# Value matmuls placed behind projection steps, norms cut in two, fill work at one rate over a chunk

## The chip, the cores and the metric

The kernel runs on one core of a Trainium2 chip. The metric is the device time of one execution in microseconds; the median of three runs is 2244.29 us (2243.23 to 2244.43). One further execution was recorded with the profiler and took 2247.89 us; its trace spans 2246.0 us, and every duration below comes from it.

## What is computed

Two layers over 2048 tokens of width 1024, between RMS norms. The even layer projects its input, attends over keys chosen by a top-256 index score (8 heads of 64), and runs a depthwise convolution of 31 taps with a layer norm beside it. The odd layer is a gated short convolution.

```python
def even_layer(h, pos, w_in, w_out, cb_w, cb_bias, ln_g, ln_b):
    u = h @ w_in
    q, k, v, qi, ki, wi, gate_a, glu_b, gate_b = _split(u, EVEN_SPLIT)
    ...
    a = dsa_attention(q, k, v, qi, ki, wi).reshape(Bn, S, ATT_WIDTH)
    a = a * jax.nn.silu(gate_a)
    ...
    c = causal_depthwise_conv(c, cb_w) + cb_bias
    c = jax.nn.silu(layer_norm(c, ln_g, ln_b))
    c = c * jax.nn.silu(gate_b)
    return jnp.concatenate([a, c], axis=-1) @ w_out

def odd_layer(h, w_in, conv_w, w_out):
    b_gate, c_gate, xin, gate = jnp.split(h @ w_in, 4, axis=-1)
    y = b_gate * causal_depthwise_conv(c_gate * xin, conv_w)
    return (y * jax.nn.silu(gate)) @ w_out

for l in range(DEPTH):
    h = rms_norm(x, norm_g[l])
    x = x + (even_layer(...) if l % 2 == 0 else odd_layer(...))
return rms_norm(x, final_g)
```

## The kernel before

Tokens are cut into four chunks of 512 (16 blocks of 128). Channels lie on partitions, tokens on the free axis. Every large product is made of three f16 matmuls (`mm3`, lines 179 to 183: high times high, high times low, low times high) over eight slices of the contraction, so one 128x512 result takes 24 matmuls. One projection step loads a 1 MB weight tile and makes two such results: 48 matmuls.

The program has two halves. The first (to about 856 us) projects the input of the even layer, scores and selects keys, and does the attention of chunk 0 and the convolution of chunk 0. The second goes chunk by chunk (the loop at line 1172). For a chunk `c` it runs 24 projection steps: 4 of `out_even(c)`, which need the attention and convolution of that chunk (tiles `mh`, `ml`; the attention fills slices 0 to 3 of the contraction, the convolution slices 4 to 7); 4 of `late`, which is `out_odd` of the chunk before; and 16 of `odd(c)`. Chunk 0 has its own first steps (lines 1112 to 1124), and its 16 steps of `odd` stand in the loop. Between the steps, `weave` (line 127) calls generators that emit other work: `attend(c + 1)`, one head of one block at a call (4 blocks of 8 heads make 32 calls, and a 33rd call retires what is left), and `conv(c + 1)`, which needs 16 calls. A rate says how many calls each step makes; a fraction is carried from step to step inside one `weave` and dropped at its end. R0, R1 and R2 are the rates of the attention, CN0 and CNR those of the convolution.

A head's work is a chain through every engine. TensorE makes the scores `ps_q` (`scores`, line 1148), in segments of 512 keys; VectorE adds the mask and keeps a running minimum (line 335); ScalarE takes the exponential (342) and casts (344); GpSimd makes the low part (345); SyncE issues one DMA transpose a segment (347, tile `pt`); then TensorE multiplies by the values (`values_of`, line 368, tile `ps_v`). The values of a head are emitted two calls after its scores (`LOOK` is 2). After the eighth head of a block, `end` (line 376) scales the result, transposes it on TensorE (390), multiplies by the gate (392) and splits it into `mh` and `ml`.

The order on each engine comes from a scheduler that works with a timeline of its own. It may place an instruction anywhere its inputs allow. `paced` (line 119) ties an instruction behind the last projection matmul emitted before the call (`state["gate"]`): it may not stand ahead of it on the engine. The first scores of a head are paced; the value matmuls are not. Each engine executes its instructions in the order given, and TensorE waits at a matmul whose inputs have not arrived.

`row_rstd` (line 152) makes a norm: four small matmuls sum squares, VectorE does a Newton iteration on 4 numbers, and one more matmul (line 163) spreads the result over the partitions.

Of the kernel before, what the change touches and what calls it, by code (L numbers as in the profile page):

```python
# [43 lines left out]
NWT = 2  # L44
LOOK = 2
ATR = 3.5
CE, CX, CN0, CNR, R0, R1, R2 = 1.5, 3.0, 1.0, 1.0, 2.0, 2.0, 2.5
ORDER = ('ggqgqg', 'ggqgqg', 'gggg', 'qq')
EX = 1
TQ, TP = 2, 4  # L50
# [23 lines left out]
def trunk_kernel(ctx: ExitStack, tc: tile.TileContext, xT, pos, wE, woE, wO, woO, par, tab, outT):  # L74
# [39 lines left out]
    w_dr = {}  # L114
    URGENT = {(wE.tensor.name, t) for t in (T_K, T_QI, T_KI)}

    state = {"mm": None, "gate": None, "scanned": False}

    def paced(ins):
        if state["gate"] is not None:  # L120
            tc.add_manual_dep(ins.ins, state["gate"].ins.name, mybir.DependencyInfo(mybir.DependencyClass.NoSync, mybir.DependencyReason.DATA), reason="pace")
# [5 lines left out]
    def weave(main, steps=99, *fills):  # L127
        owed = [0.0] * len(fills)
        for n, _ in enumerate(main):
            state["gate"] = state["mm"]  # L130
            for i, (gen, rate) in enumerate(fills):
                owed[i] += rate
                while owed[i] >= 1.0:
                    owed[i] -= 1.0
                    next(gen, None)
            state["gate"] = None
            if n + 1 == steps:
                break
# [11 lines left out]
        return r  # L150

    def row_rstd(pool, ps_pool, sq, inv_n, out_scale, n=TT):
        st = ps_pool.tile([P, CH], FP32, name="ps_m")
        for i in range(n):
            T.matmul(out=st[:, i:i + 1], lhsT=sq[:, i * P:(i + 1) * P], rhs=ones[:, 0:1], start=True, stop=True)
        a = pool.tile([P, TT], FP32, name="rs_a")[:, 0:n]
        V.tensor_scalar(out=a, in0=st[:, 0:n], scalar1=inv_n, scalar2=EPS, op0=ALU.mult, op1=ALU.add)
        r = newton_rsqrt(pool, a, [P, TT], "rs")[:, 0:n]
        dg = pool.tile([P, TT, P], FP32, name="rs_d", bufs=1)
        state["rstd"] = V.scalar_tensor_tensor(out=dg[:, 0:n, :], in0=id32.rearrange("p (o t) -> p o t", o=1).broadcast_to([P, n, P]), scalar=out_scale,  # L160
                                               in1=r.rearrange("p (i o) -> p i o", o=1).broadcast_to([P, n, P]), op0=ALU.mult, op1=ALU.mult)
        rb = ps_pool.tile([P, CH], FP32, name="ps_m")
        T.matmul(out=rb[:, 0:n * P], lhsT=ones, rhs=dg[:, 0:n, :].rearrange("p i t -> p (i t)"), start=True, stop=True)  # L163
        return rb

    def square_into(pool, acc, t, first, eng, tile=None):
# [12 lines left out]
    def mm3(out, sh, sl, mh, ml):  # L179
        for k in range(KD):  # L180
            T.matmul(out=out, lhsT=sh(k), rhs=mh(k), start=k == 0, stop=False)  # L181
            T.matmul(out=out, lhsT=sh(k), rhs=ml(k), start=False, stop=False)  # L182
            state["mm"] = T.matmul(out=out, lhsT=sl(k), rhs=mh(k), start=False, stop=k == KD - 1)  # L183

    def weight(pool, stage_pool, src, t):
        key = (src.tensor.name, t)
# [35 lines left out]
    def conv_norm(c, pool, aux, ps_pool, sink, sums=None):  # L222
        cv = pool.tile([P, NJ, CH], FP32, name="cv")
        s = pool.tile([P, CH], FP32, name="cn_s")
        cb, lng, lnb = pr("cb"), pr("lg"), pr("lb")
        for j in range(NJ):
            ci = pool.tile([P, CK - 1 + CH], FP32, name="cin")
            SP.dma_start(out=ci, in_=cg_dr[j][:, c * CH:c * CH + CK - 1 + CH])
            out = cv[:, j, :]
            acc = sums() if sums else out  # L230
            paced(A.activation(out=acc, in_=ci[:, 0:CH], func=AF.Identity, scale=cwt[:, j, 0:1], bias=cb[:, j:j + 1]))  # L231
            for t in range(1, CK):
                ins = V.scalar_tensor_tensor(out=out if t == CK - 1 else acc, in0=ci[:, t:t + CH], scalar=cwt[:, j, t:t + 1], in1=acc, op0=ALU.mult, op1=ALU.add)  # L233
                if t % 8 == 1:
                    paced(ins)
                if t % 8 == 0:
                    yield
            if j == 1:
                G.tensor_tensor(out=s, in0=cv[:, 0, :], in1=out, op=ALU.add)
            elif j > 1:  # L240
                G.tensor_tensor(out=s, in0=s, in1=out, op=ALU.add)
        mu = ps_pool.tile([P, CH], FP32, name="ps_m")
        T.matmul(out=mu, lhsT=inv512, rhs=s, start=True, stop=True)
        ssq = pool.tile([P, CH], FP32, name="cn_q")
        for j in range(NJ):
            V.tensor_tensor(out=cv[:, j, :], in0=cv[:, j, :], in1=mu, op=ALU.subtract)
            square_into(aux, ssq, cv[:, j, :], j == 0, G)
        with tc.high_priority(PRI):
            rb = row_rstd(aux, ps_pool, ssq, 1.0 / CW, 1.0)
        for j in range(NJ):  # L250
            x = cv[:, j, :]
            V.tensor_tensor(out=x, in0=x, in1=rb, op=ALU.mult)
            A.activation(out=x, in_=x, func=AF.Identity, scale=lng[:, j:j + 1], bias=lnb[:, j:j + 1])
            th = pool.tile([P, CH], FP32, name="cn_s")
            A.activation(out=th, in_=x, func=AF.Tanh, scale=0.5)
            V.scalar_tensor_tensor(out=x, in0=th, scalar=1.0, in1=x, op0=ALU.add, op1=ALU.mult)
            gb = pool.tile([P, CH], FP32, name="cn_q")
            SP.dma_start(out=gb, in_=gb_dr[c][:, j, :])
            V.scalar_tensor_tensor(out=x, in0=x, scalar=0.5 * SM, in1=gb, op0=ALU.mult, op1=ALU.mult)
            sink(j, x)  # L260
            yield
# [49 lines left out]
    def attention(blocks, tiles, scores, context, vv, eng, look, sink):  # L311
# [39 lines left out]
        def values_of(blk, h, parts):  # L351
            b, i = blk["b"], h % group
            if i == 0:
                state["av"] = context()
            if h == 0:
                blk["an"] = tiles["a"]()
                blk["ga"] = tiles["ga"]()
                SP.dma_start(out=blk["ga"], in_=ga_dr[b])
            av, an = state["av"], blk["an"]
            for kt, hi, lo in parts:  # L360
                if b < TT:
                    T.matmul(out=av, lhsT=hi, rhs=vv[:, kt, 0, :], start=kt == 0, stop=False)
                    T.matmul(out=av, lhsT=hi, rhs=vv[:, kt, 1, :], start=False, stop=False)
                    T.matmul(out=av, lhsT=lo, rhs=vv[:, kt, 0, :], start=False, stop=kt == b)
                    continue
                order = ((hi, 2 * HD), (lo, HD)) if kt == 0 else ((lo, HD), (hi, 2 * HD))
                for n, (p, w) in enumerate(order):
                    T.matmul(out=av[:, i, 0:w], lhsT=p, rhs=vv[:, kt].rearrange("p a d -> p (a d)")[:, 0:w], start=kt + n == 0, stop=kt == b and n == 1)  # L368
            if b < TT:
                A.copy(out=an[:, h, :], in_=av)  # L370
            elif i == group - 1:
                part = an[:, h - i:h + 1, :]
                A.copy(out=part, in_=av[:, :, 0:HD])
                V.tensor_tensor(out=part, in0=av[:, :, HD:2 * HD], in1=part, op=ALU.add)
# [643 lines left out]
                square_into(l1, acc, x1[:, jt, :], jt == 0, V)  # L1018
            yield

    def norm_odd(x1, acc):
        with tc.high_priority(PRI):
            return norm_all(x1, acc)

    def norm_all(x1, acc):
        rb = row_rstd(l1, ps_n, acc, 1.0 / D, SX)
        nh = l1.tile([P, KD, CH], F16, name="nh", bufs=1)
        nl = l1.tile([P, KD, CH], F16, name="nl", bufs=1)
        for k in range(KD):
            xn = l1.tile([P, CH], FP32, name="xi")  # L1030
            V.scalar_tensor_tensor(out=xn, in0=x1[:, k, :], scalar=g1[:, k:k + 1], in1=rb, op0=ALU.mult, op1=ALU.mult)
            split(nh[:, k, :], nl[:, k, :], xn)
        return nh, nl
# [86 lines left out]
    even = out_even(0, *m[0], x1, acc)  # L1120
    weave(even, EX, (cnv, CX))
    drain(even)
    n = norm_odd(x1, acc)
    drain(late)


# [45 lines left out]
    for c in range(NCH):  # L1172
        att = attend(c + 1) if c + 1 < NCH else iter(())
        if c > 0:
            cnv = conv(c + 1) if c + 1 < NCH else iter(())
            x1, acc = rows()
            weave(out_even(c, *m[c], x1, acc), 99, (cnv, CNR), (att, R0))
            n = norm_odd(x1, acc)
            weave(late, 99, (cnv, CNR), (att, R1))
        yh = l1.tile([P, KD, CH], F16, name="yh", bufs=1)  # L1180
        yl = l1.tile([P, KD, CH], F16, name="yl", bufs=1)
        weave(odd(*n, yh, yl), 99, (cnv, CNR if c else CN0), (att, R1 if c else R2))
        late = out_odd(c, x1, yh, yl, 2 if c + 1 == NCH else 1)
        drain(att)
        drain(cnv)
# [71 lines left out]
```

## Time and profile before

| | us |
|---|---|
| median of 3 runs | 2244.29 |
| profiled execution | 2247.89 |
| its span | 2246.0 |
| TensorE busy | 1994.7 |
| VectorE busy | 1657.6 |
| ScalarE busy | 1180.3 |
| GpSimd busy | 811.3 |

TensorE is busy for 89% of the span, the others for less. A matmul's recorded duration is longer than the distance to the next one, since matmuls overlap; idle time is what is read here. The second half consists of a stage for each chunk's steps: 932 to 1205 us (the 16 steps of `odd(0)`, with the attention of chunk 1), 1205 to 1553 us (24 steps, attention of chunk 2), 1553 to 1890 us (24 steps, attention of chunk 3), and a last one with no fill work.

### The profile page before, as it was taken

What the parts mean: (1) busy time and instruction counts of PE and PEld (TensorE: products, weight loads), DVE (VectorE), ACT (ScalarE), POOL (GpSimd) and SP (SyncE); (2) the same over time, 40 slices, a digit from 0 to 9 for tenths busy, and PEclk for the clock granted to TensorE, in tenths of its full rate; (3) what the DMA queues carried; (4) which work ended last, traced back from release to release, by engine and by line L of the source; (5) the groups of instructions that cost most, each with busy time, mean ns of one, the idle gap of its engine ahead of it and who ended that gap; (6) DMA issues with size and microseconds to landing.
All of it is one profiled execution on the core that took longest, in us unless ns stands there. A gap on an engine that the chain in (4) does not pass through costs nothing. (4 is left out here: it accounts for less than half of the span.)

```text
span 2246.0 us, 34960 instructions
## 1 busy us (share of the span) xinstructions
PE 1994.7 (89%) x12252; PEld 1069.3 (48%) x12252; DVE 1657.6 (74%) x3580; ACT 1180.3 (53%) x2409; POOL 811.3 (36%) x761
## 2 busy tenths in 40 slices
PE   5777888888999898888879999999899999999997
PEld 4544464555464543343334444444454444444446
DVE  7999979998887877878665888753798874243224
ACT  5656655567567855475764665641655682121111
POOL 4755443534151502264652554510534561000000
PEclk9989999999999999999999999999999999999999
DMA  6445456334754476677885788862878985324224
GB/s 238 158 163 190 167 170 228 118 103 144 214 137 139 139 225 214 222 197 186 194 210 184 185 212 204 182 164 105 179 159 193 213 183 140 118 99 145 99 97 166
DMA packets 406052, 380.89 MB, mean 170 GB/s; under 512 B 313456, under 2 KB 333680, under 8 KB 385136
## 3 DMA queue, kind: packets, MB, share of 16 engines
q1 hardware_dynamic: 405872, 378.63, 59.8%
q8 instruction: 96, 1.57, 0.3%
q14 instruction: 84, 0.69, 0.1%
HBM read 216.45 MB, written 88.70 MB: 136 GB/s over the span
## 5 line engine op out<-in xcount | busy, mean ns | idle before, releaser
L345 POOL TENSOR_TENSOR pp<-lg,pp 128x512 f16<-128x512 f32 (+3 forms) x320 | 348.4, 1110 | 550.4 <-ACT pp L344 471.5
L181 PE MATMUL ps_w<-nh,wt 128*128 128x512 f16 x1024 | 393.0, 385 | 19.8 <-ACT wt L201 17.6
L182 PE MATMUL ps_w<-nl,wt 128*128 128x512 f16 x1024 | 393.7, 385 | 0.0
L183 PE MATMUL ps_w<-nh,wt 128*128 128x512 f16 x1024 | 389.2, 386 | 4.1 <-POOL wt L202 4.0
L181 PEld LDWEIGHTS <-wt 128*128 128x128 f16 x2112 | 208.7, 99 | 265.6 <-ACT wt L201 28.2
L183 PEld LDWEIGHTS <-wt 128*128 128x128 f16 x2112 | 208.8, 99 | 246.6 <-issue 16.0
L182 PEld LDWEIGHTS <-wt 128*128 128x128 f16 x2112 | 208.9, 99 | 240.7 <-issue 26.3
L233 DVE SCALAR_TENSOR_TENSOR ps_c<-cin,cwt,ps_c 128x512 f32<-128x512 f32 x348 | 260.6, 749 | 24.0 <-ACT ps_c L231 20.7
L342 ACT ACTIVATE lg<-lg,m 128x512 f32<-128x512 f32 (+3 forms) x320 | 206.9, 648 | 119.5 <-DVE m L335 119.0
L202 POOL TENSOR_TENSOR wt<-w_stage,wt 128x512 f16<-128x512 f32 x136 | 169.4, 1251 | 255.4 <-ACT wt L201 241.3
L181 PE MATMUL ps_p<-xh,wt 128*128 128x512 f16 x480 | 185.2, 387 | 16.0 <-ACT th L214 5.6
L344 ACT CAST pp<-lg 128x512 f16<-128x512 f32 (+3 forms) x320 | 165.9, 549 | 47.0 <-DMA pt<-pp 42.4
L183 PE MATMUL ps_p<-xh,wt 128*128 128x512 f16 x480 | 184.1, 386 | 1.9 <-POOL wt L202 1.9
L182 PE MATMUL ps_p<-xl,wt 128*128 128x512 f16 x480 | 185.0, 385 | 0.0
L725 PE MATMUL ps_i<-ki,qst 128*128 128x512 f16 (+3 forms) x608 | 146.9, 362 | 34.0 <-ACT relu L727 33.4
L368 PE MATMUL ps_v<-vv,pt 128*128 128x64 f16 (+1 forms) x2016 | 127.4, 209 | 55.0 <-DMA pt<-pp 51.9
L729 DVE SCALAR_TENSOR_TENSOR sc<-relu,wi,sc 128x1024 f32<-128x1024 f32 (+7 forms) x140 | 164.3, 1174 | 13.8 <-ACT relu L727 13.3
L727 ACT ACTIVATE relu<-ps_i 128x1024 f32<-128x1024 f32 (+7 forms) x176 | 140.9, 810 | 63.4 <-DVE sc L729 37.6
L181 PE MATMUL ps_p<-wt,xh 128*128 128x256 f16 (+1 forms) x608 | 163.9, 270 | 4.7 <-ACT u L584 2.4
L182 PE MATMUL ps_p<-wt,xh 128*128 128x256 f16 (+1 forms) x608 | 164.0, 270 | 0.6 <-POOL wt L202 0.6
L183 PE MATMUL ps_p<-wt,xl 128*128 128x256 f16 (+1 forms) x608 | 163.4, 270 | 1.2 <-DVE xl L479 1.2
L780 ACT ACTIVATE junk<-sc,t_x 128x640 bf16<-128x640 f32 (+5 forms) x84 | 118.6, 1412 | 72.1 <-DVE t_x L795 43.3
(293 smaller groups left out, 3866.9 us busy)
## 6 DMA issues: line engine op xcount, KB each, us to landing
wt<-w_in_wo_dram SPq DMA_DIRECT2D x48, 1024.0 KB, 4.8
wt<-w_in_we_dram SPq DMA_DIRECT2D x39, 1024.0 KB, 5.6
w_stage<-in_wo_dram SPq DMA_DIRECT2D x64, 256.0 KB, 3.4
w_in_wo_dram<-wt SPq DMA_DIRECT2D x16, 1024.0 KB, 5.0
wt<-w_in_woo_dram SPq DMA_DIRECT2D x16, 1024.0 KB, 4.8
w_in_we_dram<-wt SPq DMA_DIRECT2D x13, 1024.0 KB, 4.9
w_stage<-in_we_dram SPq DMA_DIRECT2D x48, 256.0 KB, 3.7
wt<-w_in_woe_dram SPq DMA_DIRECT2D x12, 1024.0 KB, 4.8
```

Of the source, the lines that this page charges most:

```text
L181: T.matmul(out=out, lhsT=sh(k), rhs=mh(k), start=k == 0, stop=False)
L182: T.matmul(out=out, lhsT=sh(k), rhs=ml(k), start=False, stop=False)
L183: state["mm"] = T.matmul(out=out, lhsT=sl(k), rhs=mh(k), start=False, stop=k == KD - 1)
L202: G.tensor_tensor(out=wt[:, 1, ks, :], in0=st, in1=wt[:, 0, ks, :], op=ALU.subtract)
L233: ins = V.scalar_tensor_tensor(out=out if t == CK - 1 else acc, in0=ci[:, t:t + CH], scalar=cwt[:, j, t:t + 1], in1=acc, op0=ALU.mult, op1 ...
L342: A.activation(out=e, in_=e, func=AF.Exp, bias=last, scale=-1.0, accum_out=blk["ss"][:, h, si:si + 1])
L344: A.copy(out=pp[:, 0:w], in_=e)
L345: eng.tensor_tensor(out=pp[:, w:2 * w], in0=e, in1=pp[:, 0:w], op=ALU.subtract)
L368: T.matmul(out=av[:, i, 0:w], lhsT=p, rhs=vv[:, kt].rearrange("p a d -> p (a d)")[:, 0:w], start=kt + n == 0, stop=kt == b and n == 1)
L725: T.matmul(out=ps[:, r0:r0 + r], lhsT=qst[:, h, i * P:(i + 1) * P], rhs=ki[:, a, s0 + r0:s0 + r0 + r], start=a == 0, stop=a == 1)
L727: A.activation(out=rl[:, 0:w], in_=ps[:, 0:w], func=AF.Relu)
L729: V.scalar_tensor_tensor(out=sc[:, s0:s0 + w], in0=rl[:, 0:w], scalar=wi[:, b, h:h + 1], in1=tiny[:, s0:s0 + w] if h == 0 else sc[:, s0:s0 ...
```

## The change

The first value matmul of each head is paced as the first scores are. The norm `row_rstd` is split into `row_diag` (sums and Newton iteration) and `spread` (the matmul over partitions); the convolution's generator yields between them, and `norm_odd` runs one step of `late`, with its fill calls, between them and ties the spread behind the first 24 matmuls of that step. The rates go from 2.0, 2.0, 2.5 heads a step to 1.45, 1.45, 2.2, and the convolution's from 1.0 to 0.9 and 0.75.

```diff
-CE, CX, CN0, CNR, R0, R1, R2 = 1.5, 3.0, 1.0, 1.0, 2.0, 2.0, 2.5
+CE, CX, CN0, CNR, R0, R1, R2 = 1.5, 3.0, 0.9, 0.75, 1.45, 1.45, 2.2
...
     def row_rstd(pool, ps_pool, sq, inv_n, out_scale, n=TT):
+        return spread(ps_pool, row_diag(pool, ps_pool, sq, inv_n, out_scale, n), n)
+
+    def row_diag(pool, ps_pool, sq, inv_n, out_scale, n=TT):
         st = ps_pool.tile([P, CH], FP32, name="ps_m")
...
+        return dg
+
+    def spread(ps_pool, dg, n=TT):
         rb = ps_pool.tile([P, CH], FP32, name="ps_m")
-        T.matmul(out=rb[:, 0:n * P], lhsT=ones, rhs=dg[:, 0:n, :].rearrange("p i t -> p (i t)"), start=True, stop=True)
+        paced(T.matmul(out=rb[:, 0:n * P], lhsT=ones, rhs=dg[:, 0:n, :].rearrange("p i t -> p (i t)"), start=True, stop=True))
         return rb
...
+        if state["first"] is None:
+            state["first"] = state["mm"]
...
-            rb = row_rstd(aux, ps_pool, ssq, 1.0 / CW, 1.0)
+            dg = row_diag(aux, ps_pool, ssq, 1.0 / CW, 1.0)
+        yield
+        with tc.high_priority(PRI):
+            rb = spread(ps_pool, dg)
...
-                    T.matmul(out=av[:, i, 0:w], lhsT=p, ...)
+                    ins = T.matmul(out=av[:, i, 0:w], lhsT=p, ...)
+                    if kt + n == 0:
+                        paced(ins)
...
-    def norm_odd(x1, acc):
+    def norm_odd(x1, acc, work, *fills):
         with tc.high_priority(PRI):
-            return norm_all(x1, acc)
-
-    def norm_all(x1, acc):
-        rb = row_rstd(l1, ps_n, acc, 1.0 / D, SX)
+            dg = row_diag(l1, ps_n, acc, 1.0 / D, SX)
+        state["first"] = None
+        weave(work, 1, *fills)
+        state["gate"] = state["first"]
+        with tc.high_priority(PRI):
+            rb = spread(ps_n, dg)
+            state["gate"] = None
+            return norm_all(x1, rb)
+
+    def norm_all(x1, rb):
...
-            n = norm_odd(x1, acc)
+            n = norm_odd(x1, acc, late, (cnv, CNR), (att, R1))
             weave(late, 99, (cnv, CNR), (att, R1))
```

The order of instructions changes from about 720 us of the trace on; ahead of that every engine's order is the same.

The first place is TensorE inside the third chunk's attention, where the values of a head begin (`nh`, `nl` and `wt` are a projection of `odd`, `qs_a` the queries of a scores matmul, `pt` the transposed weights of a head). Before:

```order
L182 LDWEIGHTS wt
L182 MATMUL ps_w<-nl,wt 128x512
L183 LDWEIGHTS wt
L183 MATMUL ps_w<-nh,wt 128x512
L368 LDWEIGHTS pt
L368 MATMUL ps_v<-vv,pt 128x128
L368 LDWEIGHTS pt
L368 MATMUL ps_v<-vv,pt 128x64
```

With the change, same engine and same part of the program:

```order
L1170 LDWEIGHTS qs_a
L1170 MATMUL ps_q<-kk,qs_a 128x512
L1170 LDWEIGHTS qs_a
L1170 MATMUL ps_q<-kk,qs_a 128x512
L379 LDWEIGHTS pt
L379 MATMUL ps_v<-vv,pt 128x128
L379 LDWEIGHTS pt
L379 MATMUL ps_v<-vv,pt 128x64
```

The values have moved from the middle of a step to its end, behind the scores of the head that the call emits.

The second place is TensorE at the end of that chunk's attention, where the last block is transposed (`ps_m<-id_62,a_nat`) for the next chunk. Before:

```order
L183 LDWEIGHTS wt
L183 MATMUL ps_w<-nh,wt 128x512
L181 LDWEIGHTS wt
L181 MATMUL ps_w<-nh,wt 128x512
L390 MATMUL ps_m<-id_62,a_nat 128x128 x4
L182 LDWEIGHTS wt
L182 MATMUL ps_w<-nl,wt 128x512
```

With the change (`mh` is the input of the next chunk's `out_even`):

```order
L379 LDWEIGHTS pt
L379 MATMUL ps_v<-vv,pt 128x64
L379 LDWEIGHTS pt
L379 MATMUL ps_v<-vv,pt 128x128
L403 MATMUL ps_m<-id_62,a_nat 128x128 x4
L187 LDWEIGHTS wt
L187 MATMUL ps_w<-mh,wt 128x512
```

The transposes of the last block, once among projections of `odd`, now follow its last values directly, and the first matmul that reads their result follows them directly.

The third place is VectorE at that same end. With the change (`m_18399` is the running minimum of the chunk's last head, `rc_a` the sums of its last block, `x_18521` the first result of the next chunk's `out_even`):

```order
L346 ISA lg,m_18399<-ps_q,mb_a,m_18399 128x512
L346 ISA m_18399 128x1
L183 TENSOR_TENSOR yl<-y,yh 128x512
L394 TENSOR_REDUCE rc_a<-ss_a 128x8
L395 RECIPROCAL rc_a<-rc_a 128x8
L398 TENSOR_SCALAR rc_a<-rc_a 128x8
L387 TENSOR_TENSOR a_nat<-ps_v,a_nat 128x256
L399 TENSOR_TENSOR a_nat<-a_nat,rc_a 128x512
L405 TENSOR_TENSOR a_nat<-ps_m,ga_a 128x512
L183 TENSOR_TENSOR ml<-a_nat,mh 128x4x128
L1030 SCALAR_TENSOR_TENSOR x_18521<-ps_w,xi 128x512 x2
```

Before, the same end of a block stood between instructions of `odd`:

```order
L374 TENSOR_TENSOR a_nat<-ps_v,a_nat 128x256
L386 TENSOR_TENSOR a_nat<-a_nat,rc_a 128x512
L1050 SCALAR_TENSOR_TENSOR cx<-ps_w,cs 128x512
L1055 SCALAR_TENSOR_TENSOR y<-cx,par_sb,y 128x512 x2
L392 TENSOR_TENSOR a_nat<-ps_m,ga_a 128x512
L1059 SCALAR_TENSOR_TENSOR y<-ps_w,y 128x512
L177 TENSOR_TENSOR ml<-a_nat,mh 128x4x128
```

With the change nothing of `odd` is left between the end of the last block and the next chunk's first result.

## Rows read from the trace of the kernel before

**Rows 1.** The page: span, and busy time, share and instructions by engine.

```profile
span 2246.0 us, 34960 instructions
PE 1994.7 (89%) x12252; PEld 1069.3 (48%) x12252; DVE 1657.6 (74%) x3580; ACT 1180.3 (53%) x2409; POOL 811.3 (36%) x761
```

**Rows 2.** Windows by stage: busy time by engine, clock, DMA share, GB/s.

```profile
932.00:1205.00 273.00, 229.23 (x1339) 108.32 (x1339) 193.37 (x357) 177.32 (x399) 147.50 (x130) 0.96 0.75 200
1205.00:1553.00 348.00, 332.14 (x2069) 167.34 (x2067) 255.53 (x514) 180.23 (x424) 130.21 (x118) 0.99 0.73 178
1553.00:1890.00 337.00, 312.08 (x2171) 164.01 (x2170) 271.94 (x563) 199.45 (x476) 151.05 (x134) 0.98 0.83 180
1890.00:2246.00 356.00, 343.26 (x1783) 174.94 (x1780) 116.97 (x226) 50.69 (x101) 0.00 (x0) 0.99 0.35 120
```

**Rows 3.** Waits of TensorE, 932 to 1205 us: total us, times, longest.

```profile
PE ps_w L181 <- ACT wt L201: 17.6, 14, 4.2
PE ps_v L368 <- DMA pt<-pp: 17.3, 16, 2.2
PE ps_w L183 <- POOL wt L202: 4.0, 7, 1.4
PE ps_v L368 <- DVE a_nat L374: 2.2, 1, 2.2
```

**Rows 4.** Waits of TensorE, 1205 to 1553 us.

```profile
PE ps_v L368 <- DMA pt<-pp: 12.4, 22, 1.5
PE ps_q L1151 <- DVE m L335: 2.7, 3, 1.5
```

**Rows 5.** Waits of TensorE, 1553 to 1890 us.

```profile
PE ps_v L368 <- DMA pt<-pp: 22.2, 28, 2.1
```

**Rows 6.** Windows of short stretches: a step's rate, and the clock after waits.

```profile
926.70:937.00 10.30, 6.82 (x14) 2.35 (x15) 7.82 (x17) 2.53 (x5) 0.00 (x0) 0.50 0.91 307
...
1336.30:1343.10 6.80, 6.34 (x20) 2.76 (x21) 5.54 (x14) 4.05 (x10) 3.73 (x5) 0.50 0.85 203
...
1500.00:1550.00 50.00, 50.00 (x235) 22.95 (x234) 14.09 (x20) 7.22 (x16) 0.00 (x0) 1.00 0.32 111
```

**Rows 7.** Timeline of TensorE: last scores of the fourth chunk's first head.

```profile
1569.38 0.28 PE L1151 MATMUL ps_q<-kk,qs_a 128*128 128x128 f16 x2
```

**Rows 8.** Timeline of SyncE: that head's four transposes.

```profile
1575.09 5.46 SPq L347 DMA_TRANSPOSE pt<-pp  x4
```

**Rows 9.** All transposes of line 347, from issue to landing.

```profile
DMA to landing us min/median/max: 2.3/3.3/8.0
```

**Rows 10.** Timeline of TensorE: scores and values of the last heads.

```profile
1853.76 0.59 PE L1151 MATMUL ps_q<-kk,qs_a 128*128 128x512 f16 x2
1854.19 1.52 PE L368 MATMUL ps_v<-vv,pt 128*128 128x128 f16 x32
...
1872.91 0.52 PE L368 MATMUL ps_v<-vv,pt 128*128 128x64 f16 x8 [0.73 <-DMA pt<-pp]
```

**Rows 11.** Timeline of TensorE: last values of a block, and its transposes.

```profile
1177.70 0.85 PE L368 MATMUL ps_v<-vv,pt 128*128 128x64 f16 x8
...
1181.41 0.60 PE L390 MATMUL ps_m<-id,a_nat 128*128 128x128 f32 x4
```

**Rows 12.** Timeline of VectorE at the end of that block.

```profile
1180.11 0.68 DVE L386 TENSOR_TENSOR a_nat<-a_nat,rc_a 128x512 f32<-128x512 f32 x1
...
1182.05 0.69 DVE L392 TENSOR_TENSOR a_nat<-ps_m,ga_a 128x512 f32<-128x512 f32 x1 [0.48 <-PE ps_m L390]
1183.48 0.71 DVE L177 TENSOR_TENSOR ml<-a_nat,mh 128x512 f16<-128x512 f32 x1 [0.74 <-ACT mh L176]
```

**Rows 13.** Timeline of ScalarE at the end of that block.

```profile
1182.83 0.61 ACT L176 CAST mh<-a_nat 128x512 f16<-128x512 f32 x1
```

**Rows 14.** Waits of TensorE, 900 to 1010 us: the norm ahead of `odd(0)`.

```profile
PE ps_m L163 <- DVE rs_d L160: 5.2, 1, 5.2
```

More of the change, by code (lines that the diff above doesn't have):

```diff
@@ L115, in trunk_kernel @@
     URGENT = {(wE.tensor.name, t) for t in (T_K, T_QI, T_KI)}
-    state = {"mm": None, "gate": None, "scanned": False}
+    state = {"mm": None, "gate": None, "first": None, "scanned": False}
     def paced(ins):
@@ L367, in values_of @@
                 for n, (p, w) in enumerate(order):
-                    T.matmul(out=av[:, i, 0:w], lhsT=p, rhs=vv[:, kt].rearrange("p a d -> p (a d)")[:, 0:w], start=kt + n == 0, stop=kt == b and n == 1)
+                    ins = T.matmul(out=av[:, i, 0:w], lhsT=p, rhs=vv[:, kt].rearrange("p a d -> p (a d)")[:, 0:w], start=kt + n == 0, stop=kt == b and n == 1)
+                    if kt + n == 0:
+                        paced(ins)
             if b < TT:
@@ L1122, in trunk_kernel @@
     drain(even)
-    n = norm_odd(x1, acc)
+    n = norm_odd(x1, acc, late)
     drain(late)
@@ L1177, in trunk_kernel @@
             weave(out_even(c, *m[c], x1, acc), 99, (cnv, CNR), (att, R0))
-            n = norm_odd(x1, acc)
+            n = norm_odd(x1, acc, late, (cnv, CNR), (att, R1))
             weave(late, 99, (cnv, CNR), (att, R1))
```

## The prediction

> **What bounds the kernel now.** The page comes first: TensorE is busy for 1994.7 of 2246.0 us, VectorE for 74%, the others for less [rows 1]. So time is won or lost only where TensorE stands still or runs at half clock. Windows by stage come next, because the change acts in the second half alone: in three stages the attention of chunks 1, 2 and 3 is woven in; in the fourth nothing is woven, and neither its order nor its time should move [rows 2]. A step without fill work runs without a gap: 235 matmuls in 50 us, 0.213 us each, so 48 make 10.2 us [rows 6].
>
> The waits of TensorE are the third view. In all three stages one wait leads or nearly leads: the value matmuls stand until the DMA transposes of their head have landed, 17.3, 12.4 and 22.2 us, together 51.9 us in 66 waits [rows 3 to 5]. In the first of them waits for converted weights come on top, 17.6 and 4.0 us [rows 3]. There are 5 us more for buffers and copies (2.2 and 2.7) [rows 3, 4].
>
> The granted clock is the fourth: 0.96, 0.99 and 0.98 over 273, 348 and 337 us [rows 2]. At half clock for twice the missing share, that is 22, 7 and 13 us, in which TensorE did half the work: about 21 us lost. A short wait is enough to begin such a stretch, as at 1336 us, and a long one too, as at 927 us [rows 6].
>
> **How late the transposes are.** For the first head of the fourth chunk the last scores end at 1569.66 us and four transposes are issued from 1575.09 on, 1.37 us each [rows 7, 8]. The last goes out near 1579.2 and with 2.3 to 3.3 us to land [rows 9] it is there 12 to 13 us after the scores. For the last head the scores end at 1854.35 and the last values start at 1872.91, on landing: 18.6 us [rows 10]. The engines were emptier at the first than at the last. My reading is 12 us unloaded, up to 18.6 us in the queues of VectorE, ScalarE and GpSimd.
>
> **The change part by part.** *Pacing and lower rates.* Nothing is added to any engine; instructions move. I counted in both orders the TensorE work between a head's last scores and its first values, at the rates of rows 6 and 10. Its median goes from 10.3 to 12.5 us in the first stage, from 14.4 to 16.8 in the second, from 14.0 to 16.5 in the third: the values come some 2.3 us later after their scores. At the same time 1.45 heads a step replace 2, so VectorE, busy for 272 of 337 us [rows 2], gets its scores and convolution more thinly. I estimate 1 to 3 us less queue in the chain. Against 13 to 15 us of chain the typical head is then in time; the heads with the shortest lead still wait. I take 6, 1 and 4 us left of the waits, 11 in all: 41 us gained. Bounds: 0, if the chain becomes as much later as the values, and 51.9.
>
> *Weights.* The first stage converts weights on ScalarE and GpSimd, and its 2.2 heads a step instead of 2.5 leave ScalarE a little more room. Most of that work is per step and not per head, so I take 5 of the 21.6 us; bounds 0 and 21.6. *Clock.* With fewer short waits fewer half-clock stretches; I take a third of the 21 us, 7; bounds 0 and 21. *Buffers and copies.* Of 5 us I take 3; bounds 0 and 5. The sum won is 56 us.
>
> On the clock the Trainium skill ("TensorE: Matmul & The Clock Gate", section "A second HAM failure mode: psum-queue depth-cycling") tells of a kernel whose frequent small gaps between matmul groups made the clock swing between its levels, with throughput lost at each swing. By that rule alone, all 21 us would go with the small waits and the time would come out 14 us lower. The stretch at 927 us follows one long wait and not many small ones [rows 6], and the change makes three long ones, so the rule does not decide here.
>
> *Norms in two halves.* The long one is ahead of `odd(0)`: TensorE waits 5.2 us at the spread matmul [rows 14]. Before, 16 projection matmuls stood between the four sums and the spread; in the new order 14 do, because the sums themselves come later. That wait stays; the others are below 2 us. I price this part at 0, with bounds of 5 either way.
>
> *The ends of the chunks.* This speaks against the change. Each weave starts its count anew, so 1.45 calls a step give 5 in the four steps of `out_even`, 1 in the norm's step, 4 in the other three of `late`, and 23 in sixteen of `odd`: 33 together, exactly what the attention needs, and the 32nd and 33rd both fall in the last step. Before, 2 a step ended it in the 17th of 24. The last head's scores, all its values and the end of its block now stand behind the last projection of the chunk, and the next matmul in the queue is the first of `out_even`, which reads their result (the second and third places in the order). Nothing is behind which to hide.
>
> For the second and third chunk's ends, about 2 us of values of two earlier heads lie between the last scores and the head's own values (32 value matmuls take 1.52 us [rows 10]). Against an unloaded chain of 12 us that is a stand of 10 us. Then the block ends: last values done at 1178.55, transposes at 1181.41, gate at 1182.05, `mh` at 1182.83 to 1183.44, `ml` at 1184.19 [rows 11 to 13]. That is 5.6 us, with 0.6 of TensorE's own: 5 us more. A stand of that size leaves the clock at half for some 5 us of work after it, as at 932 to 937 us [rows 6], 2.5 to 3 us. So 18 us for each of these two ends. At the first stage's end 40 projection matmuls (8.5 us) and some values still stand between the last scores and the last values, so only 3 us of the stand are left, and 5 and 2 with them: 10 us. Together 46 us. Bounds: the ends of blocks alone, 3 times 4.4, 13 us; with the loaded chain of 18.6 us in place of 12, two times 24 and 16, 64 us.
>
> *Ahead of 856 us.* Only the last part of the first attention and the convolution's tail change places by a few microseconds; 0, with 5 either way.
>
> **Sum.** 2247.89 us for the profiled execution, less 56, plus 46: 2237.9. The median of the runs is 3.6 us below the profiled execution, so 2234 us.
>
> **The rivals.** *Slower: the chain moves with the values.* The new order on ScalarE, GpSimd and SyncE puts a head's work later as well, the queues do not shorten, and heads still wait. For it: the waits of today are just under 1 us each although leads differ, as if values were placed at the landing. Against it: the heads come more thinly. If half of the 56 us come, 28 against 46 is 18 us lost: 2262. It decides from the point where more than 20 us of the value waits are left.
>
> *Cheap ends.* The stand at an end is short, since every engine but TensorE is idle there and the chain runs faster than any seen; half the stands and 2 us less for the clock at each leave 46 at about 25, and with the values quite in time (62 won) it gives 2244.3 - 37 = 2207. Against it: issue and landing alone are 4 x 1.37 and 2.3 us of the 12 [rows 8, 9].
>
> *Even.* Won and lost cancel, as the weights in the first stage keep ScalarE the bound there and value waits only turn into waits for weights: 10 us less won, 2244.
>
> **How the numbers follow.** Forecast 0.46 (own range 2222 to 2246), slower rival 0.22, cheap ends 0.19, even 0.13. Measured differences below 0.2% (4.5 us) cannot be told from none here. From the forecast 0.37 is faster, 0.08 within and 0.01 slower; cheap ends adds 0.19 to faster; even adds 0.03, 0.07 and 0.03; the slower rival adds 0.02 within and 0.20 slower. So 0.59 faster, 0.17 same, 0.24 slower. The range reaches from the cheap ends to the slower rival: 2206 to 2264.
>
> **What would show it.** In the changed profile the value waits should stand at 10 to 15 us away from the chunk ends, and three clusters should stand out on TensorE: a wait of about 10 us at the values and one of 2 to 3 us at each side of the block's transposes, at the second and third ends, with the clock at 0.50 behind them, and a smaller one at the first. Waits for weights should be somewhat below 21 us and the wait of 5 us at the norm still there. The prediction is wrong if an end costs less than 8 or more than 25 us, if the value waits between the ends stay above 30 us, or if the last stage is not 356 us long.

## The result and the profile after

The change made the kernel slower: 2260.21 us (median of 4 runs, 2257.97 to 2263.45) against 2244.36 for the kernel before, a ratio of 1.0072 with an interval of 1.0055 to 1.009. The forecast was 2234, faster. The run that was profiled took 2257.97 us, below its median, where the profiled one of before was above its own: the two traces are 10 us apart, the medians 16. Its page:

```profile
span 2256.2 us, 34988 instructions
PE 2000.1 (89%) x12252; PEld 1078.3 (48%) x12252; DVE 1647.6 (73%) x3580; ACT 1181.4 (52%) x2411; POOL 797.5 (35%) x761
```

The totals hardly differ from [rows 1]; no work was added or taken away. To see where the 10 us of span went, the second half is cut at the first matmul of its projection steps number 7, 23, 47 and 71 (48 projection matmuls a step). Lengths in us:

| | start of first stage | first | second | third | last | span |
|---|---|---|---|---|---|---|
| before | 932.2 | 273.2 | 347.4 | 383.3 | 309.9 | 2246.0 |
| after | 938.0 | 268.2 | 356.9 | 380.3 | 312.7 | 2256.2 |

Single executions of the kernel before, timed beside the experiments, ran from 2235 to 2252 us, so a few us between the stages of two traces show nothing by themselves.

Windows of after by these stages (columns as in [rows 2], whose third window ended at 1890 us, with the attention, and not at the stage's end at 1936); behind the dots the third stage of before in the cut of the table:

```profile
938.00:1206.20 268.20, 229.37 (x1340) 108.98 (x1340) 193.58 (x358) 176.12 (x397) 139.53 (x128) 0.95 0.74 200
1206.20:1563.20 357.00, 332.11 (x2065) 169.16 (x2065) 256.02 (x514) 179.64 (x422) 128.75 (x118) 0.96 0.68 173
1563.20:1943.50 380.30, 356.51 (x2384) 185.98 (x2384) 281.64 (x578) 203.24 (x488) 149.53 (x134) 0.97 0.73 171
1943.50:2256.00 312.50, 299.02 (x1568) 154.65 (x1567) 105.38 (x209) 43.86 (x87) 0.00 (x0) 0.98 0.35 120
...
1552.80:1936.10 383.30, 358.38 (x2386) 184.93 (x2385) 282.20 (x577) 205.10 (x488) 151.05 (x134) 0.99 0.76 169
```

The granted clock of the second and third stage, 0.96 and 0.97, is lower than before, where it was 0.99 in both. Waits of TensorE in after: the norm ahead of `odd(0)`, then the three stages, each set off by a line of dots; they answer to [rows 14] and [rows 3 to 5].

```profile
PE ps_m L169 <- DVE rs_d L163: 10.0, 1, 10.0
...
PE ps_w L187 <- ACT wt L209: 14.9, 8, 3.5
PE ps_v L379 <- DMA pt<-pp: 13.0, 11, 3.2
PE ps_w L189 <- POOL wt L210: 5.6, 10, 1.6
PE ps_m L403 <- DVE a_nat L399: 2.6, 1, 2.6
...
PE ps_v L379 <- DMA pt<-pp: 18.6, 10, 7.8
...
PE ps_v L379 <- DMA pt<-pp: 16.9, 11, 8.3
PE ps_q L1170 <- DVE m L346: 3.8, 2, 3.1
```

The value waits sum to 48.5 us, nearly the 51.9 of before, in 32 waits instead of 66. The wait at the norm doubled. The waits for converted weights (14.9 + 5.6) stayed. The timeline of TensorE at the second chunk end shows the longest value wait, without the projections of `odd` ahead of it:

```profile
1544.23 1.46 PE L1170 MATMUL ps_q<-kk,qs_a 128*128 128x512 f16 x6
1545.52 2.20 PE L379 MATMUL ps_v<-vv,pt 128*128 128x128 f16 x48
1555.49 0.82 PE L379 MATMUL ps_v<-vv,pt 128*128 128x128 f16 x8 [7.76 <-DMA pt<-pp]
1556.98 0.82 PE L379 MATMUL ps_v<-vv,pt 128*128 128x64 f16 x8 [0.67 <-DMA pt<-pp]
1558.14 0.82 PE L379 MATMUL ps_v<-vv,pt 128*128 128x64 f16 x8 [0.34 <-DMA pt<-pp]
1560.61 1.11 PE L403 MATMUL ps_m<-id,a_nat 128*128 128x128 f32 x4 [1.65 <-DVE a_nat L399]
1563.16 1.01 PE L187 MATMUL ps_w<-mh,wt 128*128 128x512 f16 x2 [1.43 <-ACT mh L182]
```

This is the end that the prediction drew. The last scores, the last values, the block's transposes and the first matmul of `out_even` follow each other and wait five times, 11.9 us in all, where before projections filled the 18.6 us from a chunk's last scores to its last values [rows 10]. The window behind it has the clock at half:

```profile
1563.10:1568.10 5.00, 4.94 (x12) 1.72 (x12) 0.69 (x1) 0.01 (x1) 0.00 (x0) 0.50 0.19 52
```

That is 2.5 us more, and the value matmuls at 0.10 us each instead of 0.05 [rows 10] add some 2 by estimate: 16 us for this end. The same sum gives 17 us at the third and 7 at the first. Predicted were 18, 18 and 10.

### The profile page after: what moved, and what is told of

The parts are those of the page before. It is cut to its first block, busy times and chain, and to the rows that moved or that the text cites. A ratio compares the mean times of both kernels' runs of the same rounds, so it can differ in the third digit from the quotient of the medians.

```text
span 2256.2 us, 34988 instructions
## 1 busy us (share of the span) xinstructions
PE 2000.1 (89%) x12252; PEld 1078.3 (48%) x12252; DVE 1647.6 (73%) x3580; ACT 1181.4 (52%) x2411; POOL 797.5 (35%) x761
## 5 line engine op out<-in xcount | busy, mean ns | idle before, releaser
L356 POOL TENSOR_TENSOR pp<-lg,pp 128x512 f16<-128x512 f32 (+3 forms) x320 | 341.5, 1091 | 605.5 <-ACT pp L355 525.0
L187 PE MATMUL ps_w<-nh,wt 128*128 128x512 f16 x1024 | 393.5, 385 | 17.2 <-ACT wt L209 14.9
L189 PEld LDWEIGHTS <-wt 128*128 128x128 f16 x2112 | 209.1, 99 | 251.4 <-POOL wt L210 19.4
L187 PE MATMUL ps_p<-xh,wt 128*128 128x512 f16 x480 | 185.3, 387 | 15.3 <-ACT th L222 5.6
L187 PE MATMUL ps_p<-wt,xh 128*128 128x256 f16 (+1 forms) x608 | 167.3, 275 | 4.7 <-ACT u L597 2.4
L188 PE MATMUL ps_p<-wt,xh 128*128 128x256 f16 (+1 forms) x608 | 167.1, 275 | 0.6 <-POOL wt L210 0.6
L379 PE MATMUL ps_v<-vv,pt 128*128 128x64 f16 (+1 forms) x2016 | 118.5, 211 | 48.7 <-DMA pt<-pp 48.5
```

The source lines that it names most:

```text
L356: eng.tensor_tensor(out=pp[:, w:2 * w], in0=e, in1=pp[:, 0:w], op=ALU.subtract)
```

## The experiments

Each group of runs was timed beside the kernel before on one chip, and each ratio is against those runs (their medians were 2244.9 to 2245.5 us). Stage lengths are cut as in the table above.

**Parts alone.** The values behind projection steps, and nothing else:

```diff
-                    T.matmul(out=av[:, i, 0:w], lhsT=p, ...)
+                    ins = T.matmul(out=av[:, i, 0:w], lhsT=p, ...)
+                    if kt + n == 0:
+                        paced(ins)
```

> The kernel before, with the first value matmul of each head paced; rates and norms as before. Theory E (the loss sits at the ends of the chunks and comes from the rates): in the order the transposes of the blocks stand where they stood before, two steps or more ahead of the chunk ends, so 2244 us within 5. Theory P (pacing itself makes the values late): value waits above 60 us in the three stages and 2250 us or more.

2239.02 us, ratio 0.9973 (0.9958 to 0.9988). The pacing is not what costs. The gain seen in its trace lies in the first stage (265.5 us); the value waits fall from 51.9 to 43.0.

The rates alone:

```diff
-CE, CX, CN0, CNR, R0, R1, R2 = 1.5, 3.0, 1.0, 1.0, 2.0, 2.0, 2.5
+CE, CX, CN0, CNR, R0, R1, R2 = 1.5, 3.0, 0.9, 0.75, 1.45, 1.45, 2.2
```

> The kernel before with the new rates alone (1.45, 1.45, 2.2 heads a step; convolution 0.9 and 0.75). Theory E: the last head of each chunk's attention stands behind the last projection, as with the whole change; three waits of some 10, 17 and 17 us by step times and about 2255 us. Theory P: without pacing the scheduler places the values early enough, 2235 to 2244 us.

2269.36 us, ratio 1.0101 (1.0082 to 1.012), worse than either theory said. Its second stage, and the value waits in it:

```profile
1211.90:1579.40 367.50, 337.95 (x2065) 170.32 (x2065) 258.71 (x515) 179.10 (x423) 128.35 (x118) 0.95 0.66 169
...
PE ps_v L368 <- DMA pt<-pp: 21.0, 13, 7.8
```

The stage takes 20 us more than before, and the longest value wait stands at its end. The loss is in the rates.

The norms alone (against the whole change):

```diff
-CE, CX, CN0, CNR, R0, R1, R2 = 1.5, 3.0, 0.9, 0.75, 1.45, 1.45, 2.2
+CE, CX, CN0, CNR, R0, R1, R2 = 1.5, 3.0, 1.0, 1.0, 2.0, 2.0, 2.5
...
-                    if kt + n == 0:
-                        paced(ins)
```

> The kernel before with the norms in two halves alone; rates and pacing as before. If the split norm ahead of odd(0) costs by itself: its wait is about 10 us instead of 5.2 and the time 2249 us. If that wait is a matter of the other parts: 5 us again and 2244 us.

2230.51 us, ratio 0.9926 (0.9903 to 0.9948). Both expectations missed: a part that I had priced at nothing wins 15 us. The first stage takes 250.7 us instead of 273.2, although it begins 10.7 us later.

The whole change, but with rates at which the attention ends ahead of the chunk's end:

```diff
-CE, CX, CN0, CNR, R0, R1, R2 = 1.5, 3.0, 0.9, 0.75, 1.45, 1.45, 2.2
+CE, CX, CN0, CNR, R0, R1, R2 = 1.5, 3.0, 0.9, 0.75, 1.75, 1.75, 2.4
```

> The whole change with 1.75 heads a step instead of 1.45 and 2.4 instead of 2.2, so that the last block's transposes stand 107 and 87 projection matmuls ahead of the ends of the second and third chunk (before: 221 and 259; with the change: none), and 42 ahead of the first's. Theory E: the 45 us at the ends go, a part of the 43 us won between them stays (20 to 30), the norm's 5 us stay: 2225 to 2240 us. Theory P or any other cause away from the ends: 2255 us or more.

2229.41 us, ratio 0.9919 (0.9899 to 0.9939), as theory E said. Three numbers turn the change from 16 us lost to 16 won.

**Which half of the norms.** First the pace and both halves with the old rates (against the whole change):

```diff
-CE, CX, CN0, CNR, R0, R1, R2 = 1.5, 3.0, 0.9, 0.75, 1.45, 1.45, 2.2
+CE, CX, CN0, CNR, R0, R1, R2 = 1.5, 3.0, 1.0, 1.0, 2.0, 2.0, 2.5
```

> The norms in halves and the paced values, with the rates of before (2.0, 2.0, 2.5 and 1.0, 1.0). If the two parts add up as they were alone (-15 and -6 us): 2222 to 2226. If the paced values gain only where the weights of the first stage are late (their -6 lay in that stage alone), nothing is left for them beside the norms: 2229 to 2233.

2230.19 us, ratio 0.9931 (0.9914 to 0.9947): beside the norms the paced values bring nothing more.

The convolution's half alone:

```diff
-            rb = row_rstd(aux, ps_pool, ssq, 1.0 / CW, 1.0)
+            dg = row_diag(aux, ps_pool, ssq, 1.0 / CW, 1.0)
+        yield
+        with tc.high_priority(PRI):
+            rb = spread(ps_pool, dg)
```

> Of the change only the convolution's norm in two halves (the yield between them). Theory X (the gain of the norms, 15 us, comes from the convolution's half: it moves VectorE and ScalarE work out of the way of the weight conversion in the first stage): 2228 to 2234. Theory W (the gain comes from the norm ahead of odd(0): it makes TensorE wait longer there, and the conversions of the next weights get ahead meanwhile): 2242 to 2248.

2225.73 us, ratio 0.9911 (0.9898 to 0.9925). And `norm_odd` alone:

```diff
-        rb = row_rstd(l1, ps_n, acc, 1.0 / D, SX)
...
+            dg = row_diag(l1, ps_n, acc, 1.0 / D, SX)
+        state["first"] = None
+        weave(work, 1, *fills)
+        state["gate"] = state["first"]
+        with tc.high_priority(PRI):
+            rb = spread(ps_n, dg)
...
```

> Of the change only norm_odd in two halves, with one step of late between them. Theory W: the wait ahead of odd(0) is about 10 us in place of 5, the waits for converted weights fall from 21.6 to below 10 us, and the time is 2228 to 2234. Theory X: the wait is longer and nothing comes back for it: 2245 to 2251.

2244.3 us, ratio 1.0001 (0.999 to 1.0012). My theory W put the gain in the wrong half; and X, which had the right half, does not have the reason: ScalarE and VectorE have nearly as much to do in the first stage as before (175.8 and 187.6 us, against 177.1 and 193.5). Waits of TensorE from 926 to 1206 us with the convolution's half, in the order of the answer:

```profile
PE ps_v L379 <- DMA pt<-pp: 16.5, 16, 2.7
PE ps_m L169 <- DVE rs_d L163: 9.9, 1, 9.9
PE ps_w L187 <- ACT wt L209: 2.9, 3, 1.3
PE ps_w L189 <- POOL wt L210: 1.7, 5, 0.6
```

With `norm_odd` alone:

```profile
PE ps_w L187 <- ACT wt L209: 16.6, 13, 3.4
PE ps_v L376 <- DMA pt<-pp: 15.8, 15, 2.7
PE ps_m L169 <- DVE rs_d L163: 6.5, 2, 5.0
PE ps_w L189 <- POOL wt L210: 4.2, 8, 1.4
```

In these two runs the waits for weights are gone where the wait at the norm is long: 4.7 us longer there, 17.0 us less here, against [rows 3, 14]. What ScalarE does during that wait shows one way in which they hang together. Timelines of the kernel before, ScalarE and GpSimd (the second weight tile of `odd(0)`; its step begins at 945.9):

```profile
938.25 0.63 ACT L200 ACTIVATE w_stage<-w_stage 128x512 f32<-128x512 f32 x1 [0.69 <-DMA w_stage<-in_wo_dram]
...
948.68 1.15 POOL L202 TENSOR_TENSOR wt<-w_stage,wt 128x512 f16<-128x512 f32 x1 [1.51 <-ACT wt L201]
```

The same of the run with the convolution's half, with TensorE's wait (the step that reads the tile begins at 954.4):

```profile
933.62 0.63 ACT L208 ACTIVATE w_stage<-w_stage 128x512 f32<-128x512 f32 x1 [6.10 <-SPq L1139]
934.80 0.62 ACT L208 ACTIVATE w_stage<-w_stage 128x512 f32<-128x512 f32 x1
...
938.00 2.04 PE L169 MATMUL ps_m<-rs_d,ones 128*128 128x512 f32 x2 [9.90 <-DVE rs_d L163]
...
950.34 1.16 POOL L210 TENSOR_TENSOR wt<-w_stage,wt 128x512 f16<-128x512 f32 x1 [0.40 <-ACT wt L209]
```

Before, the first part of this tile is scaled 6 us after `odd(0)` began at 932.2, and the last is done 3.9 us after the step began. Now two of its four parts are scaled while TensorE waits, and the last is done 2.9 us ahead of the step. Counted from the start of the trace it is done no earlier (951.5 us, before 949.8): the lead comes from the step, which begins 8.5 us later.

**Where in the program.** The yield for chunk 0's convolution alone:

```diff
-        yield
+        if c == 0:
+            yield
```

> Of the convolution's norm in two halves only that of chunk 0, which is emitted ahead of the second half of the program. In the order it moves the norm ahead of odd(0) and what follows in the first stage, and nothing behind 1205 us. Theory D (the gain of e7 comes from the start of the first stage: the wait ahead of odd(0) becomes 10 us long, the weight conversions get some 5 us more lead meanwhile, and the waits for weights go): 2226 to 2233, with the waits for converted weights below 8 us and step 22 of the second half some 12 to 16 us earlier than before. Theory L (the gain comes from the norms of chunks 1 to 3): 2243 to 2250, with a longer wait and nothing back.

2230.56 us, ratio 0.9937 (0.9919 to 0.9956). For chunks 1 to 3 alone (`c > 0`):

> The other half of e7: the convolution's norm in two halves for chunks 1 to 3 alone. Theory D: 2238 to 2245, since e7 gained 5 us behind the first stage and its first 940 us are then those of before. Theory L: 2226 to 2232.

2242.07 us, ratio 0.9987 (0.9973 to 1.0002). Theory D holds both times: the gain starts where the first stage starts. Then a longer wait without any of the change, by 11 Newton iterations in place of 3 in the norm ahead of `odd(0)`:

```diff
...
+    state["newton"] = 11
     n = norm_odd(x1, acc)
+    state["newton"] = 3
```

> The kernel before, with 8 more Newton iterations (24 instructions of 0.2 us on VectorE, 4.8 us in all) in the one norm ahead of odd(0), and nothing of the change. The wait there grows from 5.2 to about 10 us. Theory D (what the change gains in the first stage is lead for the weight conversions, bought with a longer wait): faster than before although work is added, 2228 to 2238, waits for converted weights below 10 us. Theory O (the gain is in the order of the first stage's instructions as the split leaves it, and the wait is a loss): 2247 to 2251.

2233.54 us, ratio 0.9951 (0.9934 to 0.9969): work was added to the path, and the kernel is 11 us faster. Waits of TensorE from 926 to 1206 us in this run:

```profile
PE ps_v L369 <- DMA pt<-pp: 18.8, 12, 3.0
PE ps_m L164 <- DVE rs_d L161: 13.5, 2, 9.7
PE ps_w L182 <- ACT wt L202: 4.7, 4, 2.2
PE ps_w L182 <- ACT nh L177: 4.5, 1, 4.5
PE ps_w L184 <- POOL wt L203: 0.9, 3, 0.4
```

Weights 5.6 us in place of 21.6 again. The wait that grew is not the norm's alone: the first matmul of `odd(0)` stands 4.5 us for `nh`, because ScalarE has two parts of the second weight tile ahead of the casts to `nh` and stands until 938.2 for the raw weights. `odd(0)` begins at 940.6, 8.4 us later than before.

One thing is not separated: a later start of `odd(0)` also leads the scheduler to another order in the first stage. The block transposes stand up to 48 projection matmuls later in this run and with the convolution's half, and on ScalarE two parts of the second weight tile stand ahead of the casts to `nh`, where before five casts came first. Whether the lead alone would do it was not tried. At the rates of the change both together are not enough: it has the same order on ScalarE there and the second tile done 4.0 us ahead of its step, and still waits 20.5 us for weights.

**The rates one by one.** The whole change, with out_even's rate up and the first stage's at 2.4:

```diff
-CE, CX, CN0, CNR, R0, R1, R2 = 1.5, 3.0, 0.9, 0.75, 1.45, 1.45, 2.2
+CE, CX, CN0, CNR, R0, R1, R2 = 1.5, 3.0, 0.9, 0.75, 2.5, 1.45, 2.4
```

> The whole change, with two of its rates raised so that no chunk's attention reaches the chunk's last projection: R0, the rate in the four steps of out_even, 2.5 in place of 1.45, and R2 2.4 in place of 2.2; R1 stays 1.45 in the other 20 steps. The last transposes then stand 100 projection matmuls (21 us) ahead of the end of chunks 1 and 2 (of the loop) and 42 (9 us) ahead of the first end. Theory E (the change loses its time at the three ends, and the even pace itself is harmless): 2260 less about 40 us, 2215 to 2225, at least as good as the uniform 1.75 (2229). Rival P (1.45 heads a step is itself bad, since TensorE gets fewer, longer waits and a lower clock): 2240 to 2255.

2229.22 us, ratio 0.9934 (0.9921 to 0.9947): 4 us above E's range and clear of P's, 31 us better than the whole change, but not better than a uniform 1.75. With out_even's rate alone up (the rest as in the change):

```diff
-CE, CX, CN0, CNR, R0, R1, R2 = 1.5, 3.0, 0.9, 0.75, 1.45, 1.45, 2.2
+CE, CX, CN0, CNR, R0, R1, R2 = 1.5, 3.0, 0.9, 0.75, 2.5, 1.45, 2.2
```

> The whole change with one number undone: 2.5 heads a step in place of 1.45 in the four steps of out_even. The ends of chunks 1 and 2 of the loop (the second and third end) then have 100 projection matmuls behind the last transposes, and the first end stays as in the change. Theory E (the two ends cost 35 us in the trace of the change, and the even pace costs nothing): 2222 to 2230. If 1.45 a step is harmful besides (clock, buffers) or the ends are less than they look: 2235 to 2250.

2239.65 us, ratio 0.998 (0.9965 to 0.9996). Undoing the two ends gives back 20.6 us, not 35. Windows of this run, second and third stage:

```profile
1207.80:1551.90 344.10, 329.07 (x2065) 166.53 (x2065) 251.98 (x511) 179.25 (x420) 125.82 (x118) 0.98 0.71 176
1551.90:1924.70 372.80, 355.26 (x2385) 184.10 (x2384) 285.44 (x577) 203.34 (x488) 147.30 (x134) 0.99 0.76 174
```

And its waits in these two stages:

```profile
PE ps_v L379 <- DMA pt<-pp: 9.8, 12, 1.3
PE ps_q L1170 <- DVE m L346: 3.2, 2, 2.5
...
PE ps_v L379 <- DMA pt<-pp: 8.9, 11, 2.7
PE ps_q L1170 <- DVE m L346: 7.4, 6, 3.1
```

Without the ends the clock is back at 0.98 and 0.99, so most of its fall belongs to them and not to the even pace. The two stages are 3.3 and 10.4 us shorter than before. But the norms and the paced values at the old rates have them at 344.5 and 384.3 us; against that the even attention is worth some 11 us in the third stage and nothing clear in the second. Value waits go from 34.6 to 18.7 us, and waits of the scores for VectorE come up from 4.2 to 10.6.

The other undone rate: 2.5 in place of 2.2 heads a step in the first stage:

```diff
-CE, CX, CN0, CNR, R0, R1, R2 = 1.5, 3.0, 0.9, 0.75, 1.45, 1.45, 2.2
+CE, CX, CN0, CNR, R0, R1, R2 = 1.5, 3.0, 0.9, 0.75, 1.45, 1.45, 2.5
```

> The whole change with one number undone: 2.5 heads a step in place of 2.2 in the first stage. The last transposes of that stage then stand 48 projection matmuls (10 us) ahead of its end. Theory E: the first end is worth 10 us, 2250. If the waits for converted weights (20.5 us in the change) come from the 2.2 as well, because the heads then reach into the last steps of the stage: 2236 to 2243, with these waits below 10 us.

2244.06 us, ratio 0.9996 (0.9979 to 1.0014), 16 us better than the whole change and one above the second range. Its first window, and its waits in that stage:

```profile
941.80:1193.60 251.80, 223.81 (x1341) 109.47 (x1341) 189.53 (x356) 175.47 (x394) 140.26 (x128) 0.97 0.82 212
```

```profile
PE ps_v L379 <- DMA pt<-pp: 21.3, 17, 3.4
PE ps_w L187 <- ACT wt L209: 2.4, 2, 2.1
PE ps_w L189 <- POOL wt L210: 1.7, 4, 0.6
```

The stage is 16.4 us shorter than in the whole change, and the waits for weights are 4.1 us instead of 20.5. So at 2.2 the stage pays for its end and also loses the lead that the wait ahead of it had bought. It loses it on the way: the last part of the fourth tile is done 4.3 us behind the start of its step in the whole change and 3.7 here, that of the seventh to the tenth 10.2 to 14.5 us behind it against 4.1 to 7.4. Nor do later block transposes make the difference, for the third stands 559 projection matmuls into the stage here, 576 before and 636 in the whole change. The convolution's 0.9 is not it; with 1.0 and 2.2 heads:

```diff
-CE, CX, CN0, CNR, R0, R1, R2 = 1.5, 3.0, 0.9, 0.75, 1.45, 1.45, 2.2
+CE, CX, CN0, CNR, R0, R1, R2 = 1.5, 3.0, 1.0, 0.75, 1.45, 1.45, 2.2
```

> The whole change with one number undone: 1.0 convolution calls a step in place of 0.9 in the first stage; its attention stays at 2.2, so the first end stays. If the waits for converted weights come from the convolution, which at 0.9 lies beside later heads: 2246 to 2252. If they come from the attention's 2.2: 2257 to 2263.

2262.39 us, ratio 1.0082 (1.0058 to 1.0106). By which queue the 2.2 costs the lead stays open.

**Put together.** The convolution's half and the paced values, with the old rates in the first stage (against the whole change, and `norm_odd` as before):

```diff
-CE, CX, CN0, CNR, R0, R1, R2 = 1.5, 3.0, 0.9, 0.75, 1.45, 1.45, 2.2
+CE, CX, CN0, CNR, R0, R1, R2 = 1.5, 3.0, 1.0, 0.75, 2.5, 1.45, 2.5
```

> What the runs speak for, put together: the convolution's norm in two halves, norm_odd as before, the paced values, the old rates in the first stage (2.5 and 1.0), and in the others 2.5 heads a step in out_even and 1.45 in the rest, with 0.75 for the convolution, so that no chunk's attention reaches the chunk's end. From the parts: 16 us of e7 in the first stage, and 5.5 and 10.5 us of e5 in the second and third, 2245 less 32: 2213 (2208 to 2220). If the gains do not add up, since the later stages gain only once: 2221 to 2228.

2221.44 us, ratio 0.9893 (0.9874 to 0.9913): the lowest, ahead of both kernels, though the gains add up only in part and its interval overlaps that of the convolution's half alone. Its second and third stage:

```profile
1191.40:1533.40 342.00, 327.65 (x2066) 167.01 (x2065) 254.39 (x513) 179.69 (x423) 128.85 (x118) 0.99 0.73 181
1533.40:1910.10 376.70, 357.62 (x2386) 185.19 (x2385) 283.67 (x577) 204.28 (x488) 148.38 (x134) 0.98 0.74 172
```

The second stage is as long as with the convolution's half alone (342.0 us) and the third 6.9 us shorter (383.6).

## Why the prediction was wrong

*The step that failed* is the size of what is won: "in the typical head is then in time", with 11 us of value waits left, 41 won. 48.5 us are left. Of these the three ends hold 19.8 (1.2, 8.8 and 9.9), which the sum had booked among the 46; the other 28.7 us lie away from them, where 11 were predicted. The estimates under the step were not far off: the chain from a head's last scores to its last landing fell in the median from 13.8 to 13.1, 15.7 to 13.8 and 17.5 to 15.3 us (1 to 3 had been estimated), and the values were emitted some 2.3 us later by count. The typical head is in time. But I went from medians to a sum of waits, and the heads that remain late were priced too low. Before, 43 heads wait, 1.2 us each on average; in the change 18 wait away from the ends, 1.6 us each. Of the nine of them in the second and third stage seven have a chain of 16.0 to 19.4 us, above the medians; no run says what makes these chains long. With the rates of before, paced or not, there are 52 to 67 waits of 0.75 to 0.83 us on average (paced values alone, norms alone, both). With two ends taken out, 18.7 of 34.6 us were left in the two later stages (undone `R0`), not 5, and another 6.4 came up at the scores. The forecast's own warning sign, more than 30 us between the ends, was just missed; the rival's, more than 20 us left, was met.

*The sum.* Against it 18 us of value waits, 4 of weights, 7 of clock and 3 of buffers were not won, 5 were lost at the norm, and the ends cost 6 less: 31 us, where the medians missed by 26. The terms do not add up exactly, as the undone ends show too.

*Ends.* Right in place and mechanism, 40 us by the waits and the clock in the trace against 46. What they cost in the balance is less: 20.6 us came back for two ends that the trace puts at 33, so placing those heads earlier costs time there.

*Weights and the norm* were wrong together. I booked 5 us of weights to the lower rate and nothing to the norms. The wait ahead of `odd(0)` grew from 5.2 to 10.0 us, as the bound of 5 allowed. It grew by the convolution's half and not by `norm_odd` (9.9 and 5.0 us alone). The count of 14 matmuls in place of 16 was right, but VectorE takes up the sums 5.3 us after TensorE began them (924.66 after 919.33), before 2.6 (921.71 after 919.10). And the norms pay: alone they win 15 us. In the whole change the 2.2 heads a step took the gain away again. Both terms came out small, for reasons that were not in the sum.

*Clock.* Seven us were to be won; instead the granted clock fell to 0.96 and 0.97, mostly by the ends. With the ends undone the value waits of the second stage fell from 22 to 12, and the clock was 0.98 after 0.99. The Trainium skill ("TensorE: Matmul & The Clock Gate", section "A second HAM failure mode: psum-queue depth-cycling") tells of a kernel in which frequent small gaps between matmul groups made the clock swing and cost throughput. No gain by that rule is seen here.

*Rivals.* The slower one named 2262, and 2260 was measured; that it came so near is in part luck, since its mechanism holds in part only: heads still waited, but the chain did shorten, a little, and the loss by clock and the gain of the norms were not in it. "Even" had the weights right: in the first stage they stayed. Cheap ends fell: at the second end the chain took 12.4 us against 12 unloaded, and TensorE stood 8.8 us of it at the values, against 10 forecast and half of that in this rival. Its 25 us for the ends do not follow from its words either: half the stands of 10, 10 and 3 us and 2 less at each end leave 28.5 of the 46.

*Last stage.* Its 312.7 us are 2.8 more than before, of which the low clock behind the third end explains 1.8 (0.64 in its first 5 us). The forecast's sign of 356 us cannot be read as it was meant: it counted 46 us of the third chunk's steps behind the attention's end, which the change fills.

## What to carry to other kernels

Do not price a wait before you have seen what the other engines do meanwhile: here five runs in which a stage that converts weights just in time began 8 to 11 us later, in another order, were 11 to 19 us faster; with 2.2 heads a step in that stage the gain was lost. Fill work that is spread evenly over a stage needs slack at the stage's end, since its last chain stands with nothing to hide it (7, 16 and 17 us here); fix the end first, then the pace. And a median lead against a median chain says nothing of the sum of the waits: count the late heads, and how late each is.

## What the runs showed of the hardware

Much of the wait ahead of `odd(0)` is not the norm's arithmetic. VectorE, in the kernel before, and in the run with the convolution's half:

```profile
925.68 0.17 DVE L144 TENSOR_SCALAR rs_r<-rs_a 128x4 int32<-128x4 int32 x1 [3.82 <-DVEq L1128]
```

```profile
935.62 0.52 DVE L149 SCALAR_TENSOR_TENSOR rs_r<-rs_t,rs_r 128x4 f32<-128x4 f32 x1 [4.66 <-DVEq L1139]
```

The line named is the branch on a flag that VectorE itself has just written (`with tc.If(rv > 0)`): the engine stands 3.8 us at it where TensorE waits 5.2, ahead of the Newton iteration, and 4.7 us where TensorE waits 9.9, in the middle of it. ScalarE stood 6.1 us at the same line in the second run. What makes the branch slow no run shows. I had read [rows 14] as the cost of the norm. An iteration's small instructions on 4 numbers took 0.16 us each, one every 0.20 us, in both runs.
